# A decoder trunk on one core: four stationary weight units of a bank group run together, and a new order of W_out's units

## The chip, the core and the metric

The kernel runs on one NeuronCore of a Trainium2 chip. It is written in Bass with the Tile framework: TensorE (PE) multiplies, VectorE (DVE), ScalarE (ACT) and GpSimd (POOL) do the rest, SyncE (SP) issues most of the loads. The metric is device time in microseconds of one execution, the median of several. For the kernel before, three runs gave 988.68, 988.68 and 989.23 us, so the median is 988.68 us.

## What is computed

A trunk of two layers over 256 tokens of width 1024, all in float32. Each layer is a feed-forward block (half weight), a token mixer, and a second feed-forward block; the mixer of the first layer is a gated linear recurrence (RG-LRU), that of the second is attention with forget gates. Cut to what matters here:

```python
D_MODEL, SEQ, DEPTH, D_FF, D_RNN = 1024, 256, 2, 2816, 1344

def swiglu(x, w_gate, w_up, w_down):
    return (jax.nn.silu(x @ w_gate) * (x @ w_up)) @ w_down

def recurrent_block(x, w_in, conv_w, conv_b, w_a, b_a, w_x, b_x, lam, w_out):
    gx = x @ w_in
    gate, rec = gx[..., :D_RNN], gx[..., D_RNN:]
    rec = causal_depthwise_conv(rec, conv_w, conv_b)
    rec = rg_lru(rec, w_a, b_a, w_x, b_x, lam)
    return (jax.nn.gelu(gate) * rec) @ w_out

for layer in range(DEPTH):
    if layer == 1:
        k, v, c = shared_kv(h, kv_norm_g, w_kv, w_fgate, b_fgate)
    f = swiglu(rms_norm(h, ffn1_pre_g[layer]), ffn1_w_gate[layer], ffn1_w_up[layer], ffn1_w_down[layer])
    h = h + 0.5 * rms_norm(f, ffn1_post_g[layer])
    hn = rms_norm(h, mix_pre_g[layer])
    m = recurrent_block(hn, ...) if layer == 0 else forgetting_attention(hn, w_q, w_o, k, v, c)
    h = h + rms_norm(m, mix_post_g[layer])
    f = swiglu(rms_norm(h, ffn2_pre_g[layer]), ffn2_w_gate[layer], ffn2_w_up[layer], ffn2_w_down[layer])
    h = h + 0.5 * rms_norm(f, ffn2_post_g[layer])
```

## The kernel before

**Three products for one.** Each float32 matrix is split into an upper part (rounded to the type float32r) and a lower part (the rest), and x @ w is computed as upper·upper + upper·lower + lower·upper.

**Units.** The weights come in units of 128 x 1024 numbers (512 KB). `split` (line 195) makes the two parts of a unit: ACT copies the raw load into `whi` (line 204), DVE subtracts it from the raw load into `wlo` (line 205). There are five buffers for raw loads (`RAW`) and nine each for `whi` and `wlo` (`WB`). All units stand in one list, `items`, 333 long. `prepare_next` (line 387) issues the next unit's load and split; it does so only when the unit nine places back is marked as done. `slot(t, i)` (line 406) prepares unit i if that has not happened yet, runs its work, marks it as done, and calls `tick`. A `tick` (line 113) counts down the deferred jobs, runs those that are due, and lets `prepare_next` take one unit. A job that is marked calm waits while `state["edge"]` is true.

**Orders.** Only PE's order is the order in which the program is written; for the other engines the framework orders the instructions. Each engine then works through its own queue in order. SP issues the loads in the order of the units.

**Two ways of multiplying.** In `mm3` (line 210) the activations are the stationary operand and 512 columns of weights move past, three products for each piece, for one half t of the tokens (128 rows) at a time. It serves W_down, W_out, the value and query projections and others. In `mmj` (line 227), the weights are stationary: a 128 x 128 block of a unit's upper part is loaded, and 512 columns move past (the upper and the lower part of x for all 256 tokens, line 239); later a block of the unit's lower part is loaded and 256 columns move past (the upper part of x alone, line 245).

**Bank groups.** 512 output columns of a gate, up or key matrix take four units of two k-blocks each, and four PSUM banks (`still`, line 524): banks 4 to 7 for gate, 0 to 3 for up, in turn. When the last unit of a group is through, `post` reads the banks: `total` (lines 519 and 520) adds the halves, and further ACT and DVE instructions make the hidden activations. `grouped` (line 546) decides how many units are run at once: the work of a unit may return `[i]` without running, and the next unit's work then runs both. Before, units are run in pairs: 16 products of 512 columns, 16 of 256, again 16 and 16. While `hooks` holds something (the first group of the kernel, whose input is still being made) units run alone. `still` sets the edge flag for k0 of 0 and 6, and after the last unit of a group.

**W_out.** `row_items` (line 477) runs W_out with `mm3`: eleven units, for t = 0 and t = 1, six products per unit and half; units 9 and 10 are run together, bank after bank. `OUT_ORDER` (line 1011) says in which order the two halves take their units: it is a list of values of t, each standing for the next unit of that half. When a half is through, `enter` (line 310) norms the result, adds it to the stream, and defers the transposes (line 269) that make the next layer's input by three ticks; lines 277, 278 and 283 make the upper and lower part of that input. The next stage is the second feed-forward block, which begins with eight units in `mm3` form.

Of the kernel before, what the change touches and what calls it, by code (L numbers as in the profile page):

```python
# [47 lines left out]
def trunk_kernel(ctx: ExitStack, tc: tile.TileContext, A: dict, out: bass.AP):  # L48
# [54 lines left out]
    def tensor_work(n):  # L103
        pace["t"] += n * 0.445e-3
# [8 lines left out]
    def tick():  # L113
        for p in list(pend):
            p[0] -= 1
            if p[0] < 0 and not (p[2] and state["edge"]):
                pend.remove(p)
                p[1]()
        purse[0] = min(purse[0] + SHARE, SHARE)
        if state["p"] >= OPEN:  # L120
            prepare_next()
        while queue and purse[0] > 0:
            cost, _, fn = queue.pop(0)
            purse[0] -= cost
            fn()
# [101 lines left out]
    def mmj(bs, parts, ks, moving):  # L227

        o, oh = pall, pall[:, :, :S]
        if len(moving(ks[0])[0].shape) == 4:  # L230
            o = o.rearrange("p n (a t b) -> p n a t b", a=2, t=2)
            oh = oh.rearrange("p n (t b) -> p n t b", t=2)
        else:
            o = o.rearrange("p n (a b) -> p n a b", a=2)
        n = len(ks)
        for i, (k, (wh, wl)) in enumerate(zip(ks, parts)):
            tensor_work(2 * S * len(bs))
            for b, w in zip(bs, wh):
                nc.tensor.matmul(o[:, b], w, moving(k)[0], start=k == 0, stop=False)  # L239
            if n > 1 and i % 2 == 1:  # L240
                tick()
        for i, (k, (wh, wl)) in enumerate(zip(ks, parts)):
            tensor_work(S * len(bs))
            for b, w in zip(bs, wl):
                nc.tensor.matmul(oh[:, b], w, moving(k)[1], start=False, stop=k == 7)  # L245
            if i == 1 and n > 2:
                tick()


# [132 lines left out]
    state = {"p": 0, "a": 0, "b": 0, "edge": False, "look": 99}  # L382
# [4 lines left out]
    def prepare_next(must=False):  # L387

        i = state["p"]
        if not must and i >= state["a"] + state["look"]:  # L390
            return
        if i >= len(items) or i >= WB and done.get(i - WB, 0) < 2:
            assert not must, i
            return
        if i not in landed:
            landed[i] = max(landed.get(i - 1, 4.0) + LOAD, pace["t"] if i < RAW else split_at[i - RAW] + LATE)
        if landed[i] > pace["t"] and not must:
            return
        pace["t"] = max(pace["t"], landed[i])
        split_at[i] = pace["t"] + 1.0  # L400
        units[i] = items[i][0]()
        state["p"] += 1
# [3 lines left out]
    def slot(t, i):  # L406
        while state["p"] <= i:
            prepare_next(True)
        if items[i][1](t, units[i]):
            return  # L410
        done[i] = done.get(i, 0) + (1 if t is not None else 2)
        if done[i] == 2:
            units.pop(i)
        tick()
# [107 lines left out]
    hooks = {}  # L522

    def still(us, k0, b0, moving=x_moving):
        if k0 == 0:
            assert not set(held) & set(range(b0, b0 + 4)), held.keys()
            lent.update(range(b0, b0 + 4))
        n = 2 * len(us)
        state["edge"] = k0 in (0, 6)
        parts = []  # L530
        for u in us:
            for j in range(2):
                cut = [slice(j * 512 + b * P, j * 512 + b * P + P) for b in range(4)]
                parts.append(([u.hi[:, c] for c in cut], [u.lo[:, c] for c in cut]))
        run_ = 1 if hooks else n
        for j in range(0, n, run_):
            if k0 + j in hooks:
                hooks.pop(k0 + j)()
            mmj(range(b0, b0 + 4), parts[j:j + run_], range(k0 + j, k0 + j + run_), moving)
            if run_ == 1 and j == 0:  # L540
                tick()
        if k0 + n == 8:
            lent.difference_update(range(b0, b0 + 4))
        state["edge"] = k0 + n == 8

    def grouped(k0, kept, fn):

        i = len(items)

        def work(t, u):  # L550
            kept.append((i, u))
            if len(kept) < 2 and not hooks and k0 % 4 == 0:
                return [i]
            us = [v for _, v in kept]
            done_ = [j for j, _ in kept]
            del kept[:]
            fn(us, k0 + 2 - 2 * len(us))
            for j in done_[:-1]:
                done[j] = 2
                units.pop(j)  # L560
        return work
# [444 lines left out]
    for p in range(6):  # L1006
# [1 line left out]
    n_rg = len(items)  # L1008
    RG_ORDER = ("0g0 0g1 0g2 0g3 0g4 0g5 0g6 0g7 1g0 1g1 r0 1g2 r1 gw0 1g3 1g4 r2 gw1 1g5 1g6 r3 gw2 1g7 "
                "0g8 0g9 0g10 r4 gw3 r5 1g8 1g9 gw4 1g10 gw5").split()  # L1010
    OUT_ORDER = [0] * 8 + [1] * 4 + [0] * 3 + [1] * 7

    gbox = {}

# [388 lines left out]
    nxt = [n_rg, n_rg]  # L1403
    for t in OUT_ORDER:
        slot(t, nxt[t])
# [66 lines left out]
```

## Time and profile before

| | us |
|---|---|
| median of three runs | 988.68 |
| the profiled execution's own time | 988.85 |
| its span, first to last instruction | 987.1 |
| PE busy | 976.7 |
| DVE busy | 672.8 |
| ACT busy | 567.1 |
| busy of the 512-column products of stationary weights (line 239, xall) | 307.2 |
| busy of their 256-column products (line 245, xall) | 167.3 |

The profile is of one execution. A timeline row gives the start in us from the span's start, the length, engine, line, operation, the tiles written and read, the shape, how many instructions are merged into the row, and in brackets the idle time of the engine ahead of it with what ended it. Matmuls overlap: a product's record lasts longer (388 to 398 ns for 512 columns) than the distance from its start to the next one's, so distances between starts are what counts.

### The profile page before, as it was taken

The page shows a single profiled execution, that of the slowest core. Times are in us where ns is not written, and L with a number is a line of the kernel's source. Part 1 is how long each engine was busy: PE and PEld are TensorE (multiplying, and loading weights), DVE is VectorE, ACT ScalarE, POOL GpSimd, SP SyncE. Part 2 cuts the span into 40 slices and gives each one's busy share as a digit, 9 for nine tenths or more (in the row PEclk, how much of TensorE's full clock was granted, in tenths as well). Part 3 has the DMA queues.
Part 4 walks back from the last instruction along what each step waited for, and adds up shares of the span by engine and source line. Part 5 has one row for each costly group of instructions (what it writes and reads, how often), then busy time and mean ns, then how long its engine had stood idle before and what let it go on. Part 6 is the DMA issues. An engine that isn't in the chain of part 4 may idle for free.

```text
span 987.1 us, 13888 instructions
## 1 busy us (share of the span) xinstructions
PE 976.7 (99%) x5294; PEld 836.9 (85%) x5294; DVE 672.8 (68%) x791; ACT 567.1 (57%) x740; POOL 50.8 (5%) x97
## 2 busy tenths in 40 slices
PE   9999999999999999999999999999999999999997
PEld 7888888899988888888898888888887688888885
DVE  5877754668997766664697676764488867667542
ACT  6666543559986655543565555553467665555431
POOL 3300000100003000000000000000030000000000
PEclk9999999999999999999999999999999999999999
DMA  8877546565337766646478666554585157666531
GB/s 276 258 273 228 186 165 191 169 181 159 109 105 230 234 192 186 199 152 179 118 218 273 196 177 192 189 198 162 171 293 177 43 172 236 200 183 193 166 111 43
DMA packets 94088, 182.06 MB, mean 184 GB/s; under 512 B 11822, under 2 KB 33414, under 8 KB 93894
## 3 DMA queue, kind: packets, MB, share of 16 engines
q1 hardware_dynamic: 93350, 181.10, 58.2%
q8 instruction: 41, 0.67, 0.3%
q0 software_dynamic: 640, 0.07, 0.1%
q14 instruction: 25, 0.20, 0.1%
q10 hardware_dynamic: 32, 0.01, 0.0%
HBM read 180.09 MB, written 1.06 MB: 184 GB/s over the span
## 4 chain that ended last, share of the span: by engine, by line
PE 72%; issue 21%; DVE 3%; ACT 3%; POOL 1%; DMA 0%; DVEq 0%; POOLq 0%; SPq 0%; ACTq 0%
PE pall L239 25%; PE pall L245 13%; PE pall L212 9%; PE pall L214 9%; PE pall L213 9%; PE pall L889 1%; PE pall L219 1%; PE pall L220 1%; PE pall L221 1%; DVE wlo L205 1%; PE pall L1198 1%; PE pall L1225 1%; POOL rstd L255 1%; ACT whi L204 0%; ACT junk L260 0%
## 5 line engine op out<-in xcount | busy, mean ns | idle before, releaser
L205 DVE TENSOR_TENSOR wlo<-raw,whi 128x1024 fp32r<-128x1024 f32 (+4 forms) x328 | 389.1, 1206 | 239.3 <-ACT whi L204 114.2
L204 ACT ACTIVATE whi<-raw 128x1024 fp32r<-128x1024 f32 (+4 forms) x328 | 341.0, 1046 | 276.8 <-PE pall L239 128.4
L239 PE MATMUL pall<-xall,whi 128*128 128x512 f32 x1280 | 307.2, 392 | 0.4 <-DVE xall L1322 0.4
L239 PEld LDWEIGHTS pall<-xall,whi 128*128 128x128 f32 x1280 | 235.1, 188 | 46.4 <-DVE xall L1322 0.9
L245 PEld LDWEIGHTS pall<-xall,wlo 128*128 128x128 f32 x1280 | 164.5, 191 | 6.7 <-DVE wlo L1330 0.4
L245 PE MATMUL pall<-xall,wlo 128*128 128x256 f32 x1280 | 167.3, 283 | 0.0
L212 PE MATMUL pall<-whi,hid 128*128 128x512 f32 (+2 forms) x400 | 153.2, 383 | 0.0
L214 PE MATMUL pall<-whi,hid 128*128 128x512 f32 (+2 forms) x400 | 152.6, 382 | 0.3 <-DVE hid L283 0.3
L213 PE MATMUL pall<-wlo,hid 128*128 128x512 f32 (+2 forms) x400 | 152.6, 381 | 0.0
L214 PEld LDWEIGHTS pall<-whi,hid 128*128 128x128 f32 x400 | 75.1, 188 | 14.2 <-DVE hid L283 0.6
L212 PEld LDWEIGHTS pall<-whi,hid 128*128 128x128 f32 x400 | 75.2, 188 | 13.6
L213 PEld LDWEIGHTS pall<-wlo,hid 128*128 128x128 f32 x400 | 75.2, 188 | 13.6
L253 POOL TENSOR_SCALAR nv<-ss 128x1 f32<-128x1 f32 x24 | 10.5, 436 | 922.0 <-ACT junk L260 921.8
L212 PE MATMUL pall<-whi,xall 128*128 128x512 f32 (+2 forms) x144 | 57.3, 398 | 0.0
L214 PE MATMUL pall<-whi,xall 128*128 128x512 f32 (+2 forms) x144 | 55.3, 384 | 0.0
L213 PE MATMUL pall<-wlo,xall 128*128 128x512 f32 (+2 forms) x144 | 55.0, 382 | 0.0
L214 PEld LDWEIGHTS pall<-whi,xall 128*128 128x128 f32 x144 | 27.1, 188 | 5.4 <-DVE xall L283 0.3
L212 PEld LDWEIGHTS pall<-whi,xall 128*128 128x128 f32 x144 | 27.1, 188 | 4.9
L519 ACT ACTIVATE sil<-pall 128x1024 f32<-128x1024 f32 (+1 forms) x22 | 20.9, 949 | 17.9 <-PE pall L245 17.8
L519 ACT ACTIVATE prod<-pall 128x1024 f32<-128x1024 f32 (+1 forms) x22 | 20.8, 948 | 17.7 <-PE pall L245 17.7
L213 PEld LDWEIGHTS pall<-wlo,xall 128*128 128x128 f32 x144 | 27.2, 189 | 4.5
L323 DVE SCALAR_TENSOR_TENSOR t<-pall,rstd,gb 128x512 f32<-128x512 f32 x16 | 11.9, 750 | 26.7 <-ACT junk L260 26.7
(193 smaller groups left out, 978.2 us busy)
## 6 DMA issues: line engine op xcount, KB each, us to landing
raw<-in_ffn_w_down_dram SPq DMA_DIRECT2D x88, 512.0 KB
raw<-in_ffn_w_up_dram SPq DMA_DIRECT2D x80, 512.0 KB
raw<-in_ffn_w_gate_dram SPq DMA_DIRECT2D x78, 512.0 KB
raw<-in_rg_w_in_dram SPq DMA_DIRECT2D x20, 504.0 KB
raw<-in_ffn_w_gate_dram SPq DMA_DIRECT2D x20, 256.0 KB
raw<-in_rg_w_out_dram SPq DMA_DIRECT2D x10, 504.0 KB
raw<-in_ffn_w_up_dram SPq DMA_DIRECT2D x16, 256.0 KB
raw<-in_w_kv_dram SPq DMA_DIRECT2D x8, 512.0 KB
```

The costliest lines, as they stand in the source:

```text
L204: nc.scalar.activation(hi[:parts, c:c + m], rawv[:, c:c + m], AF.Copy)
L205: nc.vector.tensor_tensor(lo[:parts, c:c + m], rawv[:, c:c + m], hi[:parts, c:c + m].bitcast(F32), ALU.subtract)
L212: nc.tensor.matmul(ps, xh, wh, start=first, stop=False)
L213: nc.tensor.matmul(ps, xh, wl, start=False, stop=False)
L214: nc.tensor.matmul(ps, xl, wh, start=False, stop=last)
L219: nc.tensor.matmul(ps, wh, xh, start=first, stop=False)
L220: nc.tensor.matmul(ps, wh, xl, start=False, stop=False)
L239: nc.tensor.matmul(o[:, b], w, moving(k)[0], start=k == 0, stop=False)
L245: nc.tensor.matmul(oh[:, b], w, moving(k)[1], start=False, stop=k == 7)
L253: nc.gpsimd.tensor_scalar(v, ss[:, 0:1], ss[:, 1:2] if n == 2 else 0.0, D * EPS * f * f, ALU.add, ALU.add)
L323: nc.vector.scalar_tensor_tensor(t1[n], pf[n], r_in, gb[:, n * 512:(n + 1) * 512], ALU.mult, ALU.mult)
L519: nc.scalar.activation(v, pall[:, b:b + m, S:], AF.Copy)
```

## The change

The four units of a bank group are run in one call (the condition under which a unit is held is now `k0 < 6`), so that a group is 32 products of 512 columns and then 32 of 256. `mmj` ticks after every second unit-block in both passes but the last, and drops the edge flag from the second tick on. `OUT_ORDER` gives t = 1 a fifth unit before t = 0 takes its last three.

```diff
@@ mmj
             if n > 1 and i % 2 == 1:
                 tick()
+                if i > 1:
+                    state["edge"] = False
         for i, (k, (wh, wl)) in enumerate(zip(ks, parts)):
             tensor_work(S * len(bs))
             for b, w in zip(bs, wl):
                 nc.tensor.matmul(oh[:, b], w, moving(k)[1], start=False, stop=k == 7)
-            if i == 1 and n > 2:
+            if i % 2 == 1 and i < n - 1:
                 tick()
@@ grouped
         def work(t, u):
             kept.append((i, u))
-            if len(kept) < 2 and not hooks and k0 % 4 == 0:
+            if k0 < 6 and not hooks:
                 return [i]
@@
-    OUT_ORDER = [0] * 8 + [1] * 4 + [0] * 3 + [1] * 7
+    OUT_ORDER = [0] * 8 + [1] * 5 + [0] * 3 + [1] * 6
```

## The prediction

> **What bounds the kernel now.** I read the page first (busy time and granted clock), then the list of PE's waits, then the timeline of PE at the places that the change touches, and last the queues that feed it.
>
> ```profile
> PE 976.7 (99%) x5294; PEld 836.9 (85%) x5294; DVE 672.8 (68%) x791; ACT 567.1 (57%) x740; POOL 50.8 (5%) x97
> PEclk9999999999999999999999999999999999999999
> ```
>
> ```profile
> engine line waited for: us in total, times, longest us
> PE pall L156 <- DVE idle L144: 1.5, 1, 1.5
> PE pall L1225 <- DVE pe L1218: 1.0, 2, 0.7
> PE pall L239 <- DVE xall L1322: 0.4, 1, 0.4
> PE pall L363 <- DVE hn L356: 0.3, 1, 0.3
> PE pall L214 <- DVE hid L283: 0.3, 1, 0.3
> PE pall L214 <- DVE y L974: 0.2, 1, 0.2
> ```
>
> PE is busy for 976.7 of 987.1 us at full clock, and its listed waits sum to 3.7 us, 1.5 of them the start. So a regrouping of products can win only what lies in the distances between products and in these few waits. It can lose much more: by making PE wait for units that come too late.
>
> ```profile
> L205 DVE TENSOR_TENSOR wlo<-raw,whi 128x1024 fp32r<-128x1024 f32 (+4 forms) x328 | 389.1, 1206 | 239.3 <-ACT whi L204 114.2
> L204 ACT ACTIVATE whi<-raw 128x1024 fp32r<-128x1024 f32 (+4 forms) x328 | 341.0, 1046 | 276.8 <-PE pall L239 128.4
> L239 PE MATMUL pall<-xall,whi 128*128 128x512 f32 x1280 | 307.2, 392 | 0.4 <-DVE xall L1322 0.4
> ```
>
> These rows of the costliest groups say who waits for whom: ACT's splits stand idle 128.4 us for products of line 239, which must give back a `whi` buffer, while line 239 stands idle 0.4 us in all, and for its input, not for a split. The supply of units runs ahead up to the limit of the nine buffers.
>
> **Part 1: four units together.** It adds and removes no instruction: products, splits, loads and ticks are as many (a pair ticks 4 times, a group of four 4 + 3 + 1 = 8 times). SP's loads keep their order, which is that of the units. What changes is how often PE goes from 512 columns to 256 and back.
>
> ```profile
> 336.28 3.82 PE L239 MATMUL pall<-xall,whi 128*128 128x512 f32 x16
> ...
> 341.84 3.82 PE L239 MATMUL pall<-xall,whi 128*128 128x512 f32 x16
> 345.50 2.08 PE L245 MATMUL pall<-xall,wlo 128*128 128x256 f32 x16
> 347.41 3.82 PE L239 MATMUL pall<-xall,whi 128*128 128x512 f32 x16
> ...
> 430.91 0.40 PE L212 MATMUL pall<-whi,hid 128*128 128x512 f32 x1
> ```
>
> The timeline of the second feed-forward block. From 336.28 to 430.91 there are 17 pairs of units, (430.91 - 336.28)/17 = 5.566 us each. The 512-column pass takes 345.50 - 341.84 = 3.66 us, the 256-column pass 1.91 us (0.119 per product). A narrower window cuts the pass that starts at 341.84:
>
> ```profile
> 342.77 2.89 PE L239 MATMUL pall<-xall,whi 128*128 128x512 f32 x12
> ```
>
> The first four products take 342.77 - 341.84 = 0.93 us, 0.2325 each; the other twelve 345.50 - 342.77 = 2.73 us, 0.2275 each. The start of a 512-column pass costs 0.93 - 4 x 0.2275 = 0.02 us. A group has two such starts before and one after.
>
> ```profile
> L239 PE MATMUL pall<-hid,whi x64: 387/390/478, 516.7 to 537.4; 128*128 128x512 f32 x64
> ```
>
> Groups: (1280 + 64)/32 = 42; the first runs unit by unit as before, so 41 x 0.02 = **0.8 us less**. Bounds: nothing, if the start costs more after a longer 256-column pass (0.04 after 32 as against 0.02 after 16); 1.1 us, if a steady pass goes at 0.2268 and a pair's rest over 16 x (0.2268 + 0.1194) = 5.539 us is all start cost (0.027 x 41).
>
> The Trainium skill (TensorE: Matmul & The Clock Gate, section Back-to-back issue gap) gives the distance of warm products by their columns alone, N/2.4 + 2.5 ns, thus 216 and 109 ns. The trace has 227.5 and 119 and a dearer start, so it does not agree in size. By that rule the order of products would be worth nothing, and the sum below would be without its 0.8 us.
>
> **What hides the rest of part 1.** The units of a group are marked as done at its end, not two by two, so the splits of the units nine places on are written later: the first at the group's end, three more at ticks of the next group. The first of these units is the second one of the group after the next: its upper part is needed one group and one unit's pass after that end, 11.13 + 1.84 = 13.0 us, its lower part 7.3 - 0.9 = 6.4 us later still. Even if the reading of the bank (about 3 us on ACT) goes first, a split of 1.05 leaves some 9 us for the upper part, and DVE's 1.21 more than that for the lower one. So in the long runs of groups I take it as nothing. At the start there is less cover:
>
> ```profile
> 19.72 3.82 PE L239 MATMUL pall<-xall,whi 128*128 128x512 f32 x16
> 23.37 2.08 PE L245 MATMUL pall<-xall,wlo 128*128 128x256 f32 x16
> 25.28 3.82 PE L239 MATMUL pall<-xall,whi 128*128 128x512 f32 x16
> ```
>
> ```profile
> 19.24 1.05 ACT L204 ACTIVATE whi<-raw 128x1024 fp32r<-128x1024 f32 x1
> 20.19 1.02 ACT L519 ACTIVATE sil<-pall 128x1024 f32<-128x1024 f32 x1
> 21.10 2.95 ACT L204 ACTIVATE whi<-raw 128x1024 fp32r<-128x1024 f32 x3
> 24.99 1.06 ACT L624 ACTIVATE sil<-sil 128x1024 f32<-128x1024 f32 x1 [0.94 <-DVE sil L623]
> ```
>
> The second group begins at 19.72 with units 4 and 5. Units 6 and 7 now follow at 23.37 and 25.2, not at 25.28 and 27.1. Their upper parts are the first two of the three splits from 21.10, done at 22.1 and 23.1: 1.2 and 2.1 us to spare. Their lower parts are needed later than before. I take nothing, and keep the loss for a rival.
>
> **The ticks** move inside a group. Jobs at the seventh tick (line 743 below) come after 24 of 32 products of 256 columns, where they came after 8 of the last 16: eight products ahead of the next group in both.
>
> ```profile
> 74.82 0.24 PE L743 MATMUL pall<-ident,prow 88*126 88x88 f32 x1
> ...
> 75.88 4.10 PE L239 MATMUL pall<-xall,whi 128*128 128x512 f32 x16
> 79.82 2.08 PE L245 MATMUL pall<-xall,wlo 128*128 128x256 f32 x16
> ```
>
> The next group's first pass takes 79.82 - 75.88 = 3.94, 0.28 us over 3.66, since it waits for the bank that this transpose borrowed. That stays; if it went, it would be 0.28 us more.
>
> **Part 2: W_out.**
>
> ```profile
> 291.50 0.39 PE L212 MATMUL pall<-whi,y 126*128 126x512 f32 x1
> 291.72 0.39 PE L213 MATMUL pall<-wlo,y 126*128 126x512 f32 x1
> 291.88 0.61 DVE L974 TENSOR_TENSOR y<-y,y 126x256 fp32r<-126x256 f32 x2
> 292.35 0.19 PEld L214 LDWEIGHTS pall<-whi,y 126*128 126x128 f32 x1 [0.66 <-DVE y L974]
> 292.35 0.51 PE L214 MATMUL pall<-whi,y 126*128 126x512 f32 x1 [0.24 <-DVE y L974]
> ...
> 292.69 0.40 PE L212 MATMUL pall<-whi,y 126*128 126x512 f32 x1
> ```
>
> At unit 8 of t = 0 PE waits for the lower part of y, the end of the recurrence. 291.72 to 292.35 is 0.63 us and 292.35 to 292.69 is 0.34, where 0.23 is usual: 0.40 + 0.11 = 0.51 us lost. A fifth unit of t = 1 ahead of it is 6 x 0.2275 = 1.37 us of products whose inputs (the second group of y) are long there. Line 974 ends at 292.49, and the product would now ask for it at 291.95 + 1.37 = 293.3. The wait goes whole: **0.5 us less**; at the least nothing, if DVE's order puts another split (1.2 us) in between.
>
> What is late next: the end of t = 0 moves by 1.37 - 0.51 = 0.86 us, and with it the chain of `enter` on ACT, DVE and POOL and the transposes, while the next stage begins 0.51 earlier.
>
> ```profile
> 295.94 0.39 PE L214 MATMUL pall<-whi,y 84*128 84x512 f32 x1
> 300.28 1.04 PE L269 MATMUL pall<-ident,h 128*128 128x128 f32 x8
> 304.12 1.28 DVE L283 TENSOR_TENSOR xall<-xg,xall 128x512 fp32r<-128x512 f32 x2
> 306.69 0.39 PE L212 MATMUL pall<-whi,xall 128*128 128x512 f32 x1
> ```
>
> Between the transposes and the first product on the new input 24 products of t = 1 become 18. That product moves to 306.18, and the third of its unit, the first to read a lower part, to 306.64; the first half of line 283 ends at 304.12 + 0.64 + 0.86 = 305.6. One us to spare, one split of DVE (1.2 us) ahead of it would cost 0.2. I take nothing.
>
> **Sum** against the profiled execution's own time, 988.85 (span 987.1 and 1.75 around it): 988.85 - 0.8 - 0.5 = 987.55. The median lies 0.17 lower, so the prediction is **987.4 us**, 0.13% under the time before. A difference under 0.2% (2.0 us) is about what a measurement of this kernel cannot tell from none, so this forecast counts as no change.
>
> **Rivals.**
>
> More than the sum. The new places of the splits in the queues of ACT and DVE also move the other waits of the list (1.0 + 0.3 + 0.3 us, and 0.28 us at line 743). If most of them shrink, 1 us more goes: 986.4. For it: they are all ends of DVE work that shares its queue with splits. Against it: those waits stand in attention and at the ends of passes in `mm3` form, where no bank group runs.
>
> Only one half works: a product's distance hangs on its own columns alone, so that starts of passes cost nothing and W_out's wait alone goes (988.85 - 0.5 - 0.17 = 988.2), for which speaks that 0.02 us is the last digit of the rows, against it that 17 pairs in a row show the same 5.566; or what W_out gains is lost at the next stage's input (987.9). The rule of the Trainium skill above (section Back-to-back issue gap) would give the former.
>
> The other side: the second group waits for its third and fourth unit. If ACT's order sets the copy of line 519, line 624 or another split in front of units 6 and 7, unit 6 can be late for 23.37 and unit 7 for 25.2. With line 624 (done at 26.05) and one split of 1.05 ahead, unit 7 is done at 27.1, 1.9 us late: 987.4 + 1.9 = 989.3, slower than before. It decides from 23.37 on for unit 6, and eats up the gain once a wait is over 1.3 us; for 0.2% it needs 3.3 us, thus loads that come late too. Against it: all three splits ran back to back from 21.10 on, with nothing that they waited for in between.
>
> **How the numbers follow.** The forecast 0.50 (987.0 to 987.8); more than the sum 0.24; only one half 0.13 (0.08 without the starts, 0.05 without W_out); the late second group 0.13. Faster by over 0.2% (under 986.7) is most of the second case and a tail of the first, 0.27; slower by over 0.2% is the far part of the last, 0.08; the rest, 0.65, is within. The range 986.1 to 989.2 takes in the forecast with the bounds of both parts, the two half cases, most of the second case and the near part of the last.
>
> **What would show it.** Passes of 32 products in the timeline; 11.11 us for a group where two pairs took 11.13; no wait for line 974 in the list of PE's waits, and the first product of the next stage about 0.5 us earlier against the last gate product of the recurrence. Wrong would be: a wait of line 239 or 245 for line 204 or 205 anywhere, above all from 23 to 27 us; a wait of line 214 for line 283 after W_out; a 512-column pass whose first products take more than 0.233 us each; or distances inside a long pass other than 0.2275 and 0.119.

## The result, and the profile after

The changed kernel takes 987.25 us (median of 22 runs, 986.56 to 987.73), the kernel before beside it 988.75 us (988.35 to 989.28): 1.50 us less, a ratio of 0.9984 with a 95% interval of 0.9978 to 0.9990. The prediction was 987.4 us, in a range of 986.1 to 989.2. The profiled execution took 987.45 us with a span of 985.7 (before: 988.85 and 987.1).

PE's waits in the changed kernel (line numbers below 240 stay, later ones are 2 higher: line 247 is the lower pass that was line 245):

```profile
engine line waited for: us in total, times, longest us
PE pall L156 <- DVE idle L144: 1.5, 1, 1.5
PE pall L1227 <- DVE pe L1220: 1.0, 2, 0.7
PE pall L162 <- DMA grow<-in_ffn_pre_g_dram: 0.3, 1, 0.3
PE pall L365 <- DVE hn L358: 0.3, 1, 0.3
PE pall L214 <- DVE hid L285: 0.3, 1, 0.3
```

The wait for the lower part of y (line 974, now 976) is gone, and no product of a bank group waits for a split. The rows of attention and of the row passes are what they were. New is a wait of 0.3 us at the very start, for the first load. The 0.4 us of the first group (line 239 for line 1322) is gone as well, but that is not the change's doing: a second profile of the kernel before lacks it too, and one of the groups alone still has it (both below).

The timeline of PE in the second feed-forward block, and the row of the narrower window that cuts the pass at 341.07 after its third product:

```profile
341.07 7.44 PE L239 MATMUL pall<-xall,whi 128*128 128x512 f32 x32
348.35 4.00 PE L247 MATMUL pall<-xall,wlo 128*128 128x256 f32 x32
352.19 7.44 PE L239 MATMUL pall<-xall,whi 128*128 128x512 f32 x32
```

```profile
341.77 6.75 PE L239 MATMUL pall<-xall,whi 128*128 128x512 f32 x29
```

A group takes 352.19 - 341.07 = 11.12 us, where two pairs took 2 x 5.566 = 11.13. Rounded rows are coarse for that difference. Over seven groups in a row, from 341.07 to 418.87 here and from 341.84 to 419.78 before, a group takes 11.114 and 11.134 us: 0.02 less. The first three products follow at (341.77 - 341.07)/3 = 0.233 us, the other 29 at (348.35 - 341.77)/29 = 0.2269: one dear start per group, no dearer than before.

To see where the time went, the span is cut at the same products in each kernel: first product of a bank group, of a row pass, of W_out. Lengths in us, and differences from the first profile of before:

| stretch | before | changed | difference |
|---|---|---|---|
| span's start to second group | 19.72 | 19.95 | +0.24 |
| groups 2 to 6 | 56.16 | 56.04 | -0.13 |
| groups 7 to 11 | 55.96 | 55.57 | -0.39 |
| W_out, first to last product | 32.20 | 31.62 | -0.57 |
| 9 groups, second block | 100.62 | 100.47 | -0.15 |
| 2 key groups | 22.88 | 22.83 | -0.05 |
| 11 groups, third block | 122.46 | 122.24 | -0.22 |
| 9 groups, fourth block | 100.62 | 100.46 | -0.15 |

Everything between these stretches is the same within 0.05 us. Groups 7 to 11 hold the one change that the prediction had ruled out. In order of time, PE and DVE of the changed kernel around the deferred transpose (line 743, now 745):

```profile
73.26 2.36 DVE L205 TENSOR_TENSOR wlo<-raw,whi 128x1024 fp32r<-128x1024 f32 x2 [2.54 <-ACT whi L204]
74.93 0.24 PE L745 MATMUL pall<-ident,prow 88*126 88x88 f32 x1
74.95 1.20 PE L247 MATMUL pall<-xall,wlo 128*128 128x256 f32 x8
75.54 0.24 DVE L746 COPY par<-pall 126x88 f32<-126x88 f32 x1
75.70 1.22 DVE L205 TENSOR_TENSOR wlo<-raw,whi 128x1024 fp32r<-128x1024 f32 x1
75.99 1.32 PE L239 MATMUL pall<-xall,whi 128*128 128x512 f32 x5
```

and DVE of the kernel before at the same place:

```profile
75.07 1.23 DVE L205 TENSOR_TENSOR wlo<-raw,whi 128x1024 fp32r<-128x1024 f32 x1 [2.21 <-issue]
76.22 0.24 DVE L744 COPY par<-pall 126x88 f32<-126x88 f32 x1
```

What the weight loads of line 239 waited for in the kernel before (us, times):

```profile
  DVE xall L1322: 1.4, 2
  DVE par L744: 0.4, 1
```

The transpose still lies eight products ahead of the next group. But before, the copy that gives its bank back (line 744) stood behind a split that began at 75.07, and came at 76.22, after the next group's start at 75.88; a weight load of that group waited 0.4 us for it. Now the copy comes at 75.54, as a split that began earlier ends and ahead of the next one, and the next group finds its bank free at 75.99; in the changed kernel no weight load waits for it.

W_out's unit 8 of t = 0 in the changed kernel, with the DVE row that it used to wait for:

```profile
291.64 0.61 DVE L976 TENSOR_TENSOR y<-y,y 126x256 fp32r<-126x256 f32 x2
292.64 0.39 PE L212 MATMUL pall<-whi,y 126*128 126x512 f32 x1
292.87 0.39 PE L213 MATMUL pall<-wlo,y 126*128 126x512 f32 x1
293.09 0.39 PE L214 MATMUL pall<-whi,y 126*128 126x512 f32 x1
```

The lower part is done at 292.25, the product that reads it starts at 293.09 without a gap.

### The profile page after: what moved, and what is told of

Same layout as the page of the kernel before. It is cut to its first block, busy times and chain, and to the rows that moved or that the text cites. A ratio compares the mean times of both kernels' runs of the same rounds, so it can differ in the third digit from the quotient of the medians.

```text
span 985.7 us, 13881 instructions
## 1 busy us (share of the span) xinstructions
PE 975.7 (99%) x5294; PEld 837.5 (85%) x5294; DVE 670.2 (68%) x791; ACT 563.5 (57%) x740; POOL 48.9 (5%) x97
## 3 DMA queue, kind: packets, MB, share of 16 engines
HBM read 180.09 MB, written 1.06 MB: 184 GB/s over the span
## 4 chain that ended last, share of the span: by engine, by line
PE 75%; issue 20%; DVE 2%; POOL 1%; ACT 1%; DMA 0%; DVEq 0%; POOLq 0%; ACTq 0%
PE pall L239 24%; PE pall L247 13%; PE pall L212 10%; PE pall L214 10%; PE pall L213 10%; PE pall L891 2%; PE pall L221 1%; PE pall L219 1%; PE pall L220 1%; PE pall L1200 1%; DVE wlo L205 1%; PE pall L1227 1%; POOL rstd L257 1%; ACT junk L262 0%; PE pall L1241 0%
## 5 line engine op out<-in xcount | busy, mean ns | idle before, releaser
L205 DVE TENSOR_TENSOR wlo<-raw,whi 128x1024 fp32r<-128x1024 f32 (+4 forms) x328 | 384.4, 1205 | 214.6 <-ACT whi L204 120.7
L239 PE MATMUL pall<-xall,whi 128*128 128x512 f32 x1280 | 299.7, 391 | 0.0
L239 PEld LDWEIGHTS pall<-xall,whi 128*128 128x128 f32 x1280 | 237.5, 188 | 47.8 <-DVE xall L1324 0.7
L247 PEld LDWEIGHTS pall<-xall,wlo 128*128 128x128 f32 x1280 | 159.7, 192 | 3.6
L247 PE MATMUL pall<-xall,wlo 128*128 128x256 f32 x1280 | 161.2, 283 | 0.0
L637 DVE TENSOR_TENSOR hid<-prod,hid 128x1024 fp32r<-128x1024 f32 (+1 forms) x22 | 24.8, 1128 | 25.3 <-ACT hid L636 25.3
```

The source lines that it names most:

```text
L205: nc.vector.tensor_tensor(lo[:parts, c:c + m], rawv[:, c:c + m], hi[:parts, c:c + m].bitcast(F32), ALU.subtract)
L637: nc.vector.tensor_tensor(lv, pv, hv.bitcast(F32), ALU.subtract)
```

## The experiments

Each was timed beside the kernel before on one chip. On these chips the kernel before had medians of 989.13 and 989.32 us, 0.4 and 0.6 over the 988.75 from which the expectations reckon, so the differences from the kernel beside it count. The stretches of each profile stand in the table after the first four.

**The two parts apart.** The groups alone:

```diff
-    OUT_ORDER = [0] * 8 + [1] * 5 + [0] * 3 + [1] * 6
+    OUT_ORDER = [0] * 8 + [1] * 4 + [0] * 3 + [1] * 7
```

> Four units together, with the old order of W_out's units. Theory (41 groups save one start of a 512-column pass of 0.02 us each, and the copy of line 744 gets ahead of a split, 0.28 us): W_out's wait of 0.5 us for the lower part of y is back; 987.25 + 0.5 = 987.8 us, and in the trace about 0.8 us less over the bank groups than before. Rival (a product's distance hangs on its own columns alone, and the gain was W_out's): about 988.5, with nothing gained over the bank groups.

988.18 us against 989.13, ratio 0.9988 (0.9979 to 0.9998): 0.95 less, as the theory has it (988.75 - 987.8). The order alone, on the kernel before:

```diff
-    OUT_ORDER = [0] * 8 + [1] * 4 + [0] * 3 + [1] * 7
+    OUT_ORDER = [0] * 8 + [1] * 5 + [0] * 3 + [1] * 6
```

> The kernel before with the new order of W_out's units alone. Theory: no wait for the lower part of y, 0.51 us less between the first product of W_out and the first of the next stage, everything else as before: 988.75 - 0.5 = 988.2 us. Rival (what W_out gains is given back when the next stage waits for its input): 988.7.

988.64 us against 989.13, ratio 0.9995 (0.9986 to 1.0004). The interval takes in no change, so the timed runs alone don't settle it; the profile does: its W_out is 0.57 us shorter, and so it stays to the end.

**More starts of a pass.** Each unit alone, on the kernel before:

```diff
-            if len(kept) < 2 and not hooks and k0 % 4 == 0:
-                return [i]
```

> The kernel before with each unit run alone: passes of 8 products of 512 columns and 8 of 256, four starts of a pass per group in place of two. Theory of a price of 0.02 us per start: 2 x 41 x 0.02 = 1.6 us more, 990.4 us. Rival (no price per start): 988.75.

990.39 us against 989.13, ratio 1.0014 (1.0004 to 1.0023): 1.3 more, where 1.6 was expected; that the time itself is the expected 990.4 is luck, since the kernel before is 0.4 slower on this chip. The second to fourth block have their full share. Groups 7 to 11 have none, because there the deferred transpose has moved and no weight load of line 239 waits for its copy, which takes off the 0.28 us; that groups 2 to 6 are only 0.08 longer is not explained. PE's timeline in the second block:

```profile
350.67 2.00 PE L239 MATMUL pall<-xall,whi 128*128 128x512 f32 x8
352.51 1.12 PE L245 MATMUL pall<-xall,wlo 128*128 128x256 f32 x8
353.46 2.00 PE L239 MATMUL pall<-xall,whi 128*128 128x512 f32 x8
```

A unit takes 353.46 - 350.67 = 2.79 us, four of them 11.16, 0.03 over two pairs by these rounded rows. The nine groups of the block are 0.35 us longer, 0.35/(9 x 2) = 0.019 us per added start. Products of the two widths in turn, on the changed kernel:

```diff
+        if n == 8:
+            upper = [(k, b, w) for k, (wh, _) in zip(ks, parts) for b, w in zip(bs, wh)]
+            lower = [(k, b, w) for k, (_, wl) in zip(ks, parts) for b, w in zip(bs, wl)]
+            for q in range(34):
+                if q < 32:
+                    k, b, w = upper[q]
+                    nc.tensor.matmul(o[:, b], w, moving(k)[0], start=k == 0, stop=False)
+                if q >= 2:
+                    k, b, w = lower[q - 2]
+                    nc.tensor.matmul(oh[:, b], w, moving(k)[1], start=False, stop=k == 7)
...
```

> Four units together as in the changed kernel, but products of 512 and of 256 columns in turn, each 256-column one two places behind its 512-column one. If each start of a 512-column pass has its own price of 0.02 us: 31 more starts in 41 groups, 41 x 31 x 0.02 = 25 us more, about 1012 us. Rival A (the price pays back a lag that a run of 256-column products builds up, and a single one builds none): a pair of products takes 0.233 + 0.113 = 0.346 us as in a long pass, so 986.5 to 988. Rival B (no price at all): 987.25.

991.76 us against 989.13, ratio 1.0028 (1.0018 to 1.0039), where the changed kernel has 0.9984: some 4 us over it. None of the three expectations holds. PE's timeline, the first, second and ninth product of a stretch:

```profile
349.70 0.40 PE L242 MATMUL pall<-xall,whi 128*128 128x512 f32 x1
349.93 0.28 PE L245 MATMUL pall<-xall,wlo 128*128 128x256 f32 x1
...
351.11 0.40 PE L242 MATMUL pall<-xall,whi 128*128 128x512 f32 x1
```

Four pairs take 1.41 us, 0.3525 each, where a long pass has 0.2269 + 0.1198 = 0.347. A start in such a mix costs far less than 0.02 us, but it is not free: its nine groups are 0.88 + 0.15 = 1.03 us longer than the changed kernel's, 1.03/(9 x 31) = 0.004 us per start.

| difference from before | e1 groups | e2 order | e3 units | e4 in turn | e5 four | e7 tick |
|---|---|---|---|---|---|---|
| groups 2 to 6 | -0.13 | +0.03 | +0.08 | +0.24 | +0.42 | +0.02 |
| groups 7 to 11 | -0.39 | -0.02 | +0.01 | +0.13 | +0.18 | -0.29 |
| W_out | +0.02 | -0.57 | -0.06 | -0.57 | -0.57 | -0.04 |
| 9 groups, second block | -0.15 | 0.00 | +0.35 | +0.88 | +0.61 | 0.00 |
| 2 key groups | -0.05 | 0.00 | +0.05 | +0.08 | +0.11 | 0.00 |
| 11 groups, third block | -0.22 | 0.00 | +0.44 | +0.99 | +1.03 | 0.00 |
| 9 groups, fourth block | -0.15 | 0.00 | +0.35 | +0.88 | +0.60 | 0.00 |

The two parts add up without touching each other: e1 has every group stretch of the changed kernel, e2 has its W_out.

**Four and four,** between these two:

```diff
+        if n == 8:
+            for i, (k, (wh, wl)) in enumerate(zip(ks, parts)):
+                for b, w in zip(bs, wh):
+                    nc.tensor.matmul(o[:, b], w, moving(k)[0], start=k == 0, stop=False)
+                for b, w in zip(bs, wl):
+                    nc.tensor.matmul(oh[:, b], w, moving(k)[1], start=False, stop=k == 7)
...
```

> Four units together, but after every 4 products of 512 columns their 4 of 256: eight starts of a pass in a group in place of one, with runs of 4. Passes of 8, 16 and 32 pay the same 0.02 us per start, products in turn only 0.0036 us. If the whole price falls due in the first four or five products whatever the run was, 7 x 41 x 0.02 = 5.7 us more than the changed kernel, about 993. If the price grows with the run up to 8, about 0.01 us per start, 2.9 us more, about 990. Rival (distance by a product's own columns alone): 987.25, which the passes of 8 have spoken against.

991.63 us against 989.13, ratio 1.0028 (1.0016 to 1.0040): some 4 us over the changed kernel, between the two expectations. In PE's timeline four and four take 351.13 - 349.73 = 1.40 us, against 4 x 0.347 = 1.387:

```profile
349.73 1.08 PE L240 MATMUL pall<-xall,whi 128*128 128x512 f32 x4
...
351.13 1.08 PE L240 MATMUL pall<-xall,whi 128*128 128x512 f32 x4
```

By the nine groups of the second block a start costs (0.61 + 0.15)/(9 x 7) = 0.012 us, by the eleven of the third (1.03 + 0.22)/(11 x 7) = 0.016. In the same way a start costs 0.004 us for products in turn, 0.019 to 0.020 for runs of 8, and 0.017 to 0.020 (0.15/9 and 0.22/11) for 16: from 8 on it no longer grows.

Why short runs pay less per start is not shown. Each of these kernels shortens the run of narrow products ahead of a start and the run of wide ones behind it together. The distances between single products, medians over the passes of the third block, speak for the run behind it. In a long pass (the changed kernel) the first five wide products follow at 0.233, 0.236, 0.228, 0.233 and 0.231 us, the rest at 0.227; the first narrow one follows at 0.113, the rest at 0.120. In turn, wide products follow at 0.233 and narrow ones at 0.117: each wide one pays what the first of a long pass pays, though a single narrow one stands ahead of it. Of four and four, the wide ones take 0.930 us, as the first four of a long pass do (0.930); in the second block it is 0.925. So a run may pay less merely because it ends before its five dear products are through.

**What the price hangs on.** 512 columns in the lower pass too, so that the lower parts of the weights also meet the lower parts of x:

```diff
-                nc.tensor.matmul(oh[:, b], w, moving(k)[1], start=False, stop=k == 7)
+                nc.tensor.matmul(o[:, b], w, moving(k)[0], start=False, stop=k == 7)
```

> The changed kernel with 512 columns in the lower pass too (it multiplies the lower parts of the weights with the lower parts of x as well, which the reference's result doesn't need). 1344 products become longer by 0.2275 - 0.119 = 0.1075 us, 144 us in all, so about 1132 us. What it is for is the start of the upper pass. If the price of a start comes from the change from 256 to 512 columns, the first products of an upper pass follow at 0.2275 us like all others. If it comes with the change to other weights or to a new group of banks, they follow at 0.233 again.

1130.28 us in a single run, where about 1132 was expected. PE's timeline in the second block, with the row of a narrower window:

```profile
382.06 7.42 PE L239 MATMUL pall<-xall,whi 128*128 128x512 f32 x32
389.31 7.42 PE L247 MATMUL pall<-xall,wlo 128*128 128x512 f32 x32
396.56 3.79 PE L239 MATMUL pall<-xall,whi 128*128 128x512 f32 x16
```

```profile
382.74 6.74 PE L239 MATMUL pall<-xall,whi 128*128 128x512 f32 x29
```

The first three products of an upper pass take 0.68 us, 0.2267 each, the other 29 (389.31 - 382.74)/29 = 0.2266, and both passes last 7.25 us. There is no dear start, though the weights and, at a group's start, the banks change as before: it comes with the change from 256 to 512 columns.

**The deferred transpose.** Three ticks earlier, on the kernel before:

```diff
-    defer(40, rg_params, True)
+    defer(37, rg_params, True)
```

> The kernel before with the deferred job of line 743 three ticks earlier, in the middle of a group. Theory (the next group's first pass lost 0.28 us because the copy of line 744 stood behind a split in DVE's queue when only eight products were left): the whole of it goes, 0.28 us less between the start of the seventh group and the first row pass, 988.75 - 0.28 = 988.5 us. Rival (the 0.28 us has another cause, and moves with the bank): 988.75.

988.94 us against 989.13, ratio 0.9998 (0.9988 to 1.0007): too small for the timed runs. PE and DVE in its profile:

```profile
70.56 0.24 PE L743 MATMUL pall<-ident,prow 88*126 88x88 f32 x1
70.59 3.89 PE L239 MATMUL pall<-xall,whi 128*128 128x512 f32 x16
...
72.00 0.24 DVE L744 COPY par<-pall 126x88 f32<-126x88 f32 x1
```

The copy comes 1.4 us after the transpose, still behind a split, but the bank's next user is far: groups 7 to 11 become 0.29 us shorter, out of 55.96. So the 0.28 us was the copy coming too late for the next group. What made it late in the kernel before, the split ahead of it in DVE's queue, is read from the rows above.

**Further ahead in W_out.** Six and seven units of t = 1 ahead of the last three of t = 0, on the changed kernel:

```diff
-    OUT_ORDER = [0] * 8 + [1] * 5 + [0] * 3 + [1] * 6
+    OUT_ORDER = [0] * 8 + [1] * 6 + [0] * 3 + [1] * 5   (six)
+    OUT_ORDER = [0] * 8 + [1] * 7 + [0] * 3 + [1] * 4   (seven)
```

> The changed kernel with six units of t = 1 ahead of the last three of t = 0, and five behind. Theory (the next stage's third product waits for the first half of the lower part of its input, which in the changed kernel ends 0.8 us before): that half moves by 1.36 us, PE waits 0.56 us, 987.25 + 0.56 = 987.8 us. Rival (the chain behind t = 0 has more cover than the profile shows): 987.25.

988.07 us against 989.13, ratio 0.9991 (0.9981 to 1.0000): 1.06 less, where the changed kernel has 1.50. PE and DVE at the first unit of the next stage:

```profile
306.00 1.28 DVE L285 TENSOR_TENSOR xall<-xg,xall 128x512 fp32r<-128x512 f32 x2
306.02 0.40 PE L213 MATMUL pall<-wlo,xall 128*128 128x512 f32 x1
306.74 0.50 PE L214 MATMUL pall<-whi,xall 128*128 128x512 f32 x1 [0.32 <-DVE xall L285]
```

The third product waits for the first half of line 285: 0.72 us from the second in place of 0.23, and 0.1 more after it, 0.6 us in all, as worked out (0.56). With seven:

> The changed kernel with seven units of t = 1 ahead and four behind. Theory of the hand-over: 2.73 - 0.8 = 1.9 us of waiting, and up to 0.4 more, since the transposes come 12 products behind the end of t = 0 and then wait for the stream's new value: 989.2 to 989.6 us. Rival (enough cover): 987.25.

988.28 us against 989.13, ratio 0.9991 (0.9982 to 1.0001), but 989.56 in the profiled run; 989.2 to 989.6 was expected, so the median speaks against the theory and the profile for it. So it was taken again, beside the changed kernel and the kernel before.

> Seven units of t = 1 ahead once more, for a second profile: in the first, the stage from W_out to the first bank group was 1.74 us longer than in the changed kernel, but the median of the timed runs only about 0.7 us. If the hand-over costs 1.7 us in every execution, this profile shows it again and the median is 1.7 us over that of the changed kernel beside it. If it varies from one execution to the next, the stage comes out shorter here.

> The changed kernel once more, beside the two below on one chip. If the passes' starts, the copy of line 746 and W_out's wait are all of the gain, its stages stand against those of before as in the first profile, and its median is 1.2 to 1.6 us under that of before.

Again 988.28 us, and 989.25 in the profiled run; the changed kernel beside it 987.50 (987.67 profiled), 0.9984 of before (0.9974 to 0.9993). Its gain on this chip is 1.82 us, more than the 1.2 to 1.6 expected, though the interval, 0.7 to 2.6 us, takes in both; its stretches stand as in its first profile. Both profiles of the kernel with seven show the same two waits, here those of the first:

```profile
303.16 1.32 PE L271 MATMUL pall<-ident,h 128*128 128x128 f32 x8 [0.45 <-DVE h L331]
...
307.89 0.50 PE L214 MATMUL pall<-whi,xall 128*128 128x512 f32 x1 [0.17 <-DVE xall L285]
```

From W_out's first product to the first bank group both are 1.7 us longer than the changed kernel, 0.2 less than the theory's least, but the timed runs lose only 0.8. Neither branch of the expectation holds: the stretch did not come out shorter, and the median did not lose 1.7. Why most executions lose less here than the two profiled ones is open; that more than five units ahead lose time is shown by both.

**The start.** The kernel before once more:

> The kernel before once more, for its start. In its first profile the first product of a bank group began at 6.24 us, in every later profile of any kernel at 6.65 to 7.17. If that lies in the execution (the landing of the first loads) and not in the kernel, it begins later here too; if it lies in the kernel, at 6.24 again.

It took 989.55 us in a single run:

```profile
4.24 0.26 PE L162 MATMUL pall<-ident,grow 16*128 16x16 f32 x1 [0.41 <-DMA grow<-in_ffn_pre_g_dram]
...
7.03 1.35 PE L239 MATMUL pall<-xall,whi 128*128 128x512 f32 x3
```

The first product of a group begins at 7.03 here, later than the changed kernel's 6.90, with the same wait for the first load. From the seventh group on, this profile takes 987.84 - 76.62 = 911.22 us, the first profile of before 987.11 - 75.88 = 911.23, and both profiles of the changed kernel 909.74 and 909.73: 1.49 us less whatever the start does.

## Why the prediction was right, point by point

- **Starts of passes, 0.8 us.** Right in mechanism and in sum. The group stretches give 0.13 + 0.11 (0.39 without the 0.28 of the copy) + 0.15 + 0.05 + 0.22 + 0.15 = 0.81 us; the groups alone, more starts, and one width throughout show that it is the starts. In part the size is luck, since errors in the 0.02 us cancel. By the distances of single products above, the five dear ones of a wide pass cost some 0.027 us over the steady 0.227, and the start of a narrow pass gives 0.007 back, which the prediction left out. Its steady 0.2275 was too high: it came from rounded rows that still held the fifth dear product. It had named other distances than 0.2275 and 0.119 inside a long pass as a sign of being wrong; the changed kernel has 0.227 and 0.120, but so has the kernel before, so this was a misreading and not an effect of the change.
- **No price for a longer run.** Right: a start after 32 products of 256 columns takes 0.233 us per product, as after 16.
- **The rule that distances hang on a product's own columns,** which the forecast set against its 0.8 us: the trace does not agree. With one width throughout distances are even, at 226.6 ns; with two widths the neighbour counts. The Trainium skill (TensorE: Matmul & The Clock Gate, section Back-to-back issue gap) gives N/2.4 + 2.5 ns, 216 for 512 columns, as the gap of an isolated product, and says that in a stream of weight loads and products both set the spacing. The forecast left this condition out: the section does not say that the order of products is worth nothing.
- **The splits.** Right that they are hidden. They now run in bursts, as DVE's timeline of the changed kernel shows:

```profile
338.39 4.63 DVE L205 TENSOR_TENSOR wlo<-raw,whi 128x1024 fp32r<-128x1024 f32 x4 [2.57 <-PE pall L247]
```

- Their lead over PE stays large, since they still wait for buffers that PE gives back.
- **The second group.** Right with little to spare. PE and ACT of the changed kernel:

```profile
19.95 7.44 PE L239 MATMUL pall<-xall,whi 128*128 128x512 f32 x32
...
21.33 2.95 ACT L204 ACTIVATE whi<-raw 128x1024 fp32r<-128x1024 f32 x3
25.23 1.07 ACT L626 ACTIVATE sil<-sil 128x1024 f32<-128x1024 f32 x1 [0.95 <-DVE sil L625]
```

- Unit 6 is split at 22.4 and asked for at 19.95 + 16 x 0.2275 = 23.6; unit 7 at 23.3 and 25.4. ACT's order did not change, so the rival that ended on the slower side did not come about.
- **The tick, "that stays".** Wrong by 0.28 us, in the good direction. The step counted where the transpose lies among PE's products, which is as it said, but not what stands ahead of its copy in DVE's queue. The prediction had the size and put it into a rival.
- **W_out, 0.5 us.** Right: 0.57, alone and together.
- **The hand-over behind it, one us to spare.** Right: 0.8 us, by these rows of the changed kernel,

```profile
300.85 1.04 PE L271 MATMUL pall<-ident,h 128*128 128x128 f32 x8
304.91 1.28 DVE L285 TENSOR_TENSOR xall<-xg,xall 128x512 fp32r<-128x512 f32 x2
305.89 0.40 PE L212 MATMUL pall<-whi,xall 128*128 128x512 f32 x1
306.35 0.39 PE L214 MATMUL pall<-whi,xall 128*128 128x512 f32 x1
```

- 306.35 - (304.91 + 0.64). One unit more ahead turns it into a wait of 0.6 us.
- **The sum.** 0.81 + 0.28 + 0.57 = 1.66 us, of which the later start of that execution hides 0.24 in the first pair of profiles. The median moved by 1.50 us, 0.2 more than forecast, about the share of the copy.

## What to carry to other kernels

When PE is busy throughout, a reordering of products is worth what the distances between their starts say: cut a pass into its first products and the rest, for both kinds of pass that alternate, and multiply by the number of passes. Safer still is the time of a whole period over many in a row, since single rows are rounded to half of what a start costs here. A half that waits for a slow chain can be given other work first, but each such unit also brings the next stage's input nearer to its user; here five units ahead were better than four, six or seven. A copy that frees a bank is late by whatever stands ahead of it in its queue, so work out its place there and not only its producer's.

## What the runs showed of the hardware

The price of going from 256 to 512 columns lies in the first five products of the wide pass (0.228 to 0.236 us from start to start in place of 0.227), and there is none when both passes are equally wide (0.2266 throughout). Per start it is 0.004 us with products in turn, 0.012 to 0.016 with runs of four, and some 0.02 with runs of eight and more. Whether the run of narrow products ahead or the run of wide ones behind sets it was not tried apart, nor what in PE causes it.
